# Two-layer hybrid trunk: one weight split behind each combination, u's product ahead of the fourth sum, down units behind side pairs

## The chip, the cores and the metric

The kernel runs on one core of a Trainium2 chip. The metric is the device time of one execution in microseconds. Three runs of the kernel before took 917.51, 919.23 and 922.27 us; the median is 919.23. The engines that matter here are PE (matrix multiply), ACT and DVE (elementwise work), and SP, which only issues DMA transfers. Each works through its own list of instructions in the order that was fixed when the program was built, and waits at the head of the list until what that instruction needs is there.

## The reference

```python
for l in range(DEPTH):                                   # DEPTH = 2
    f = _swiglu(_rmsnorm(h, ff1_norm_pre[l]), ff1_w_gate[l], ff1_w_up[l], ff1_w_down[l])
    h = h + 0.5 * _rmsnorm(f, ff1_norm_post[l])
    m = _hybrid_mixer(_rmsnorm(h, mix_norm_pre[l]), w_in[l], ...)   # SSD scan, pooling, block attention
    h = h + _rmsnorm(m, mix_norm_post[l])
    f = _swiglu(_rmsnorm(h, ff2_norm_pre[l]), ff2_w_gate[l], ff2_w_up[l], ff2_w_down[l])
    h = h + 0.5 * _rmsnorm(f, ff2_norm_post[l])

def _swiglu(h, wg, wu, wd):
    return (jax.nn.silu(h @ wg) * (h @ wu)) @ wd
```

There are 256 tokens of width 1024, and the hidden width of an FFN is 2816. Everything is FP32. The change lies in the four FFNs alone: FFN 1 and FFN 2 of each layer, called 01, 02, 11 and 12 below (layer, FFN).

## The kernel before

**Weights.** All weights come in units of 1 MB (a tile of 128 x 2048). SP loads a unit into one of four raw buffers (L85). To keep FP32 results, a unit is split into an upper part in the short matmul format, copied by ACT (L112, `hi`), and the remainder, subtracted by DVE (L113, `lo`). Each split goes in two pieces of 128 x 1024. The activations are split in the same way, and PE multiplies upper by upper, lower by upper and upper by lower. There are five pairs of split buffers. A fixed list of jobs says in which order units are split. `W.pump()` starts loads and splits as long as buffers are free in the program's bookkeeping, and `pump_behind(m)` does the same with the issue held behind instruction m. A scheduler then places what the program text lets it place on each engine's list, so the lists differ from the order of the text.

**FFN.** The hidden width is cut into 11 blocks of 256 columns. Blocks 0 and 1 are computed together and directly. Blocks 4, 7 and 10 are "side pairs" (`ffn_pair`): gate unit g and up unit u, each in two halves of 128 columns (`mm_side`). The blocks 2+3, 5+6 and 8+9 are computed two at a time as a "block of seven" (`ffn_quad`): instead of eight products it forms seven, from sums of weight units and sums of activations. For the block that starts at i, the splits are g1, T1, T2, T3, g2, T4 and u2. T1, T2 and T4 are sums that DVE forms in place from two raw units (L111). Between T1 and the later products, POOL issues a load that adds a further unit into a raw buffer (L117). The products (L554) are combined by DVE in four steps, "combinations" (L581, L582, L591, L592), and from there come the two hidden tiles h1 (L611) and h0 (L618). One hidden tile per block is turned on PE (`turn_tile`, L528). The other is cast by ACT (L505, `send`), transposed by a DMA that SP issues (L509), and taken in by ACT (L517).

Down units d0 to d10 (`mm_rows`, L409) multiply the turned hidden tiles and accumulate in PSUM. They are interleaved: the down units of the preceding blocks are multiplied between the products of the next one, or behind the next side pair.

**PSUM and the side pairs.** Four banks of PSUM serve the products and the pairs. In pairs 4 and 7 the order of use is g first half, g second half, the turned tile, u first half, u second half. So u's second half takes the bank of g's first half and can start only when DVE has added that half up (L362, after ACT's copy of the other part of the bank, L361). Pair 10 turns no tile on PE, and its four halves have four banks.

**The order that the change touches.** In the middle block (i = 5) the jobs run g1, T1, T2, one down unit, T3, g2, T4, u2, and the T4 product is text ahead of u2's. In the last block (i = 8) u2 comes before T4. Behind each combination `W.pump()` may start any number of splits. Behind h1 and h0 too. In the side pairs nothing holds a down unit behind the pair's u, so that the scheduler may put matmuls of a down unit between the two halves of u.

## Time and profile before

| What | Value |
|---|---|
| Runs | 917.51, 919.23, 922.27 us |
| Profiled execution | 919.46 us, span 917.8 us, mean granted clock 0.998 |
| PE busy | 906.6 us (99% of the span), 4600 matmuls |
| DVE busy | 802.0 us (87%) |
| ACT busy | 643.1 us (70%) |
| DMA | 195.74 MB, 213 GB/s on the mean |
| Chain that ended last | PE 88%, DVE 5%, DMA 3% |

Times within the span count from its start. In a row of the timeline stand the start, the time from the first start to the last end of the group, the engine, the line, the operation, the tiles written and read, the number of instructions, and in brackets the idle time before and what ended it. Neighbouring instructions overlap a little in the records: six lower-part subtractions that follow one another take 6.90 us together and 1.22 us each, so one is due every (6.90 - 1.22) / 5 = 1.136 us. FFN 01 lies at about 10 to 190 us of the span, 02 at 275 to 463, 11 at 460 to 640, 12 at 730 to 915.

### The profile page before, as it was taken

How to read it: one execution, taken by the hardware profiler on the slowest of the kernel's cores; microseconds unless marked ns; L12 is line 12 of the kernel's file. 1: busy time of each engine (PE TensorE's matmuls, PEld its weight loads, DVE VectorE, ACT ScalarE, POOL GpSimd, SP SyncE). 2: the span in 40 equal slices, each digit the busy share in tenths (PEclk: the TensorE clock that was granted, in tenths of full speed). 3: DMA queues.
4: the chain of work that ended last, by engine and by line, in shares of the span. 5: the costliest groups of instructions: out<-in, count | busy, mean ns of one | idle time of the engine just before them, and what ended most of it. 6: DMA issues, size and time to landing. Idle time of an engine off the chain costs nothing.

```text
span 917.8 us, 12327 instructions
## 1 busy us (share of the span) xinstructions
PE 906.6 (99%) x4600; PEld 764.7 (83%) x4600; DVE 802.0 (87%) x1068; ACT 643.1 (70%) x1019; POOL 29.9 (3%) x49
## 2 busy tenths in 40 slices
PE   8999999999999999999999999999999999999997
PEld 5788888889988888888888888888998888888885
DVE  6999889689868999899699989897989699989982
ACT  7767667778738776667765866777795566867681
POOL 0000000000001000000000000000000110000000
PEclk9999999999999999999999999999999999999999
DMA  8567977865534477768655958594824145959651
GB/s 352 164 249 223 365 191 273 256 228 186 183 111 168 120 287 200 275 177 320 207 194 145 343 167 288 155 338 186 297 104 165 65 172 167 348 144 299 198 176 46
DMA packets 49263, 195.74 MB, mean 213 GB/s; under 512 B 24242, under 2 KB 24754, under 8 KB 27188
## 3 DMA queue, kind: packets, MB, share of 16 engines
q1 hardware_dynamic: 47332, 182.24, 56.2%
q0 software_dynamic: 1728, 12.58, 7.5%
q8 instruction: 36, 0.59, 0.3%
q14 instruction: 23, 0.19, 0.1%
q10 hardware_dynamic: 144, 0.13, 0.0%
HBM read 188.65 MB, written 1.05 MB: 207 GB/s over the span
## 4 chain that ended last, share of the span: by engine, by line
PE 88%; DVE 5%; DMA 3%; issue 2%; ACT 1%; POOLq 0%; SPq 0%; POOL 0%; DVEq 0%; ACTq 0%
PE acc L409 27%; PE wk L554 22%; PE wk L387 13%; PE wk L356 9%; PE wk L347 6%; PE wk L358 4%; DVE lo L113 3%; PE wk L374 1%; PE wk L298 1%; DMA raw<-in_ff_q 1%; DMA raw<-in_ff_f 1%; DMA t<-t 1%; PE wk L1047 1%; DMA raw<-in_ff_d 1%; DVE raw L111 1%
## 5 line engine op out<-in xcount | busy, mean ns | idle before, releaser
L112 ACT ACTIVATE hi<-raw 128x1024 fp32r<-128x1024 f32 (+2 forms) x452 | 399.8, 937 | 128.0 <-DMA raw<-in_ff_d 41.8
L113 DVE TENSOR_TENSOR lo<-raw,hi 128x1024 fp32r<-128x1024 f32 (+2 forms) x452 | 464.2, 1077 | 20.0 <-ACT hi L112 19.3
L409 PE MATMUL acc<-hi,t 128*128 128x512 f32 x832 | 216.5, 392 | 1.0 <-ACT hi L112 0.6
L409 PEld LDWEIGHTS acc<-hi,t 128*128 128x128 f32 x832 | 154.1, 188 | 34.4 <-ACT t L247 1.8
L409 PE MATMUL acc<-lo,t 128*128 128x512 f32 x416 | 114.3, 390 | 0.0
L554 PE MATMUL wk<-hi,n 128*128 128x512 f32 x384 | 100.7, 390 | 0.0
L387 PE MATMUL wk<-hi,xT 128*128 128x512 f32 x384 | 98.8, 393 | 0.8 <-ACT hi L112 0.8
L356 PE MATMUL wk<-xT,hi 128*128 128x512 f32 x384 | 97.0, 393 | 0.0
L409 PEld LDWEIGHTS acc<-lo,t 128*128 128x128 f32 x416 | 77.6, 188 | 16.2 <-DVE lo L113 0.2
L111 DVE TENSOR_TENSOR raw<-raw,raw 128x1024 f32<-128x1024 f32 x64 | 76.4, 1217 | 11.0 <-DMA raw<-in_ff_q 11.0
L387 PEld LDWEIGHTS wk<-hi,xT 128*128 128x128 f32 x384 | 71.0, 188 | 16.8 <-ACT hi L112 2.3
L554 PEld LDWEIGHTS wk<-hi,n 128*128 128x128 f32 x384 | 71.8, 188 | 14.8
L356 PEld LDWEIGHTS wk<-xT,hi 128*128 128x128 f32 x384 | 70.0, 188 | 13.3
L554 PE MATMUL wk<-hi,xT 128*128 128x512 f32 x288 | 77.2, 389 | 0.0
L554 PEld LDWEIGHTS wk<-hi,xT 128*128 128x128 f32 x288 | 54.0, 188 | 11.4 <-DVE t L592 0.2
L358 PEld LDWEIGHTS wk<-xT,lo 128*128 128x128 f32 x384 | 52.3, 190 | 3.8
L358 PE MATMUL wk<-xT,lo 128*128 128x256 f32 x384 | 53.5, 282 | 0.0
L554 PE MATMUL wk<-lo,n 128*128 128x512 f32 x192 | 51.6, 390 | 0.5 <-DVE lo L113 0.5
L387 PE MATMUL wk<-lo,xT 128*128 128x512 f32 x192 | 51.5, 390 | 0.0
L554 PEld LDWEIGHTS wk<-lo,n 128*128 128x128 f32 x192 | 36.0, 188 | 8.4 <-DVE lo L113 0.9
L347 PE MATMUL wk<-xT,hi 128*128 128x256 f32 x320 | 42.5, 283 | 0.0
L387 PEld LDWEIGHTS wk<-lo,xT 128*128 128x128 f32 x192 | 36.0, 188 | 7.6
(185 smaller groups left out, 912.2 us busy)
## 6 DMA issues: line engine op xcount, KB each, us to landing
raw<-in_ff_q SPq DMA_DIRECT2D x48, 1024.0 KB, 6.4
raw<-in_ff_d SPq DMA_DIRECT2D x44, 1024.0 KB, 5.4
raw<-in_ff_f SPq DMA_DIRECT2D x16, 1024.0 KB, 6.4
raw<-in_ff_q POOLq DMA_DIRECT2D x12, 1024.0 KB, 8.0
raw<-in_ff_g SPq DMA_DIRECT2D x12, 1024.0 KB, 4.8
raw<-in_ff_u SPq DMA_DIRECT2D x12, 1024.0 KB, 5.0
raw<-in_w_in SPq DMA_DIRECT2D x10, 1024.0 KB, 6.0
raw<-in_w_kvz SPq DMA_DIRECT2D x8, 1024.0 KB, 6.4
```

Source lines behind the costliest of these rows:

```text
L111: nc.vector.tensor_tensor(raw[:, s], self.raw[x][:, s], self.raw[y][:, s], op=op)
L112: self.act = nc.scalar.activation(hi[:, s], raw[:, s], AF.Copy)
L113: nc.vector.tensor_tensor(lo[:, s], raw[:, s], hi[:, s].bitcast(F32), op=ALU.subtract)
L298: pre_turn.last = nc.tensor.transpose(ps[:, k * P : (k + 1) * P], xn[i][:, k * P : (k + 1) * P], ident)
L347: nc.tensor.matmul(ps, w[:, k, s], y[:, k, :], start=i == 0 and k == 0, stop=i == 2 and k == KD - 1)
L356: nc.tensor.matmul(ps, hi[:, k, s], both[:, :, k, :], start=k == 0, stop=k == KD - 1)
L358: nc.tensor.matmul(ps[:, S:], lo[:, k, s], xT[0][:, k, :], start=False, stop=k == KD - 1, skip_group_check=True)
L374: nc.tensor.matmul(ps, x[:, k, s], w[:, k, :], start=i == 0 and k == 0, stop=i == 2 and k == KD - 1)
L387: m = nc.tensor.matmul(ps, y[:, k, :], w[:, k, :], start=h == 0 and n == 0, stop=h == 1 and n == len(parts) - 1)
L409: m = nc.tensor.matmul(acc[b], x[:, j, s], w[:, j, b * 512 : (b + 1) * 512], start=first and j == 0 and i == 0, stop=last and j == 1 and i ...
L554: nc.tensor.matmul(ps, x[:, k, :], w[:, k, :], start=first and n == 0, stop=n == len(parts) - 1, skip_group_check=not first)
L1047: scan.last = nc.tensor.matmul(ps[:, s], decay[t, hd // 4][:, n * P : (n + 1) * P], xdt[t][:, s], start=True, stop=True)
```

## The change

The program text changes in five places.

1. In the middle block u2's job stands ahead of T4's, and u2's product ahead of T4's, as it was in the last block already.
2. In the middle block each pump behind a combination, behind the silu of g2 and behind h0 starts one split at most, and its issue is held behind that combination. In the last block the pump behind g2's silu is cut to four held buffers, with one split, and the one behind h0 to three held buffers. In the first block (i = 2) the pump behind h0 is held behind h0.
3. In the middle and the last block the pump behind h1 is held behind the cast that sends h1 (L505 before, L510 in the changed kernel).
4. In the first block (i = 2) the sum T2 is formed whole (L133) before its splits.
5. In the side pairs all matmuls of the down units are held behind the last matmul of u.

The matmuls are the same 4600 in both kernels, and so are the splits, the sums and the loads. What differs is their order. Line numbers rise by 2 to 12 in the changed kernel: the splits are L114 and L115, the pairs' matmuls L359 and L361, their copy and addition L364 and L365, the down units L412, the products L559, the combinations L586 to L599, silu of g2 L608, silu for h1 L619, h1 L620, h0 L630.

```diff
     def split_next(self, only=None):
+        if i in self.whole:
+            self.sum_next()
...
-    def pump(self, most=SPLIT_BUFS):
+    def pump(self, most=SPLIT_BUFS, splits=10**6):
         while True:
             if self.loaded < len(self.units) and self.live < RAW_BUFS and self.allowed > 0:
                 self.load()
-            elif self.split < len(self.jobs) and self.held < most and self.ready():
+            elif self.split < len(self.jobs) and self.held < most and splits and self.ready():
                 self.split_next()
+                splits -= 1
...
-                late = i == QUADS[-1]
+                if i == QUADS[0]:
+                    W.whole.add(p["T2", i])
+                late, swap = i == QUADS[-1], i != QUADS[0]
...
-                if late:
+                if swap:
                     p["u2", i] = W.job(u2, free=(u2,))
                 p["T4", i] = W.job(g1, (g1, ALU.add, g2), free=(g1, g2))
...
         m = nc.vector.tensor_tensor(pc, pc, w2, op=ALU.subtract)
         if late:
             pump_behind(m, SPLIT_BUFS - 1)
+        elif swap:
+            pump_behind(m, SPLIT_BUFS, 1)
         else:
             W.pump()
...
         m = nc.vector.tensor_tensor(h1, h1, pd, op=ALU.subtract)
         if late:
             pump_behind(m)
+        elif swap:
+            pump_behind(m, SPLIT_BUFS, 1)
         else:
             W.pump()
...
-        W.pump()
+        W.pump(SPLIT_BUFS - late, 1 if swap else 10**6)
...
             hf[1] = send(h1) if by_dma else h1
-            W.pump()
-
-        if not late:
+            if swap:
+                pump_behind(send.last)
+            else:
+                W.pump()
+
+        if not swap:
             second()
         product(pc, left["S4"], p["u2", i], False)
-        nc.vector.tensor_tensor(h0, pc, h0, op=ALU.mult)
+        m = nc.vector.tensor_tensor(h0, pc, h0, op=ALU.mult)
         hf[0] = send(h0) if late and by_dma else h0
-        W.pump()
+        if not late:
+            pump_behind(m, SPLIT_BUFS, 1 if swap else 10**6)
+        else:
+            W.pump(SPLIT_BUFS - 2)
+        if swap:
+            second()
         if late:
-            second()
             downs[0]()
...
-        def both(i):
-            down(i, 0)
+        def both(i, behind=None):
+            down(i, 0, behind)
...
             if i in PAIRS:
                 hT[i] = ffn_pair(i, p, turn, take, by_dma)
+                u = mm_side.end.ins
                 for b in before:
-                    both(b)
+                    both(b, u)
```

Three places show how the lists change. All are of FFN 12.

DVE, from the end of the middle block to side pair 7, before. lo_7692 is the down unit d5, lo_7718 is d6, lo_7739 is g1 of block 8; t_7579 is h1, t_7689 is h0; the two L362 rows add up the two halves of g of pair 7.

```order
766 L592 TENSOR_TENSOR t_7579<-t_7579,wk_7654 128x512
767 L113 TENSOR_TENSOR lo_7670<-raw_7595,hi_7669 128x1024
768 L113 TENSOR_TENSOR lo_7692<-raw_7597,hi_7691 128x1024 x2
769 L113 TENSOR_TENSOR lo_7718<-raw_7620,hi_7717 128x1024
770 L611 TENSOR_TENSOR t_7579<-t_7579,t_7564 128x512
771 L113 TENSOR_TENSOR lo_7718<-raw_7620,hi_7717 128x1024
772 L618 TENSOR_TENSOR t_7689<-wk_7566,t_7689 128x512
773 L113 TENSOR_TENSOR lo_7739<-raw_7652,hi_7738 128x1024 x2
774 L362 TENSOR_TENSOR t_7744<-wk_7745,t_7744 128x256
775 L362 TENSOR_TENSOR t_7744<-wk_7764,t_7744 128x256
```

The same stretch of DVE's list with the change; lo_7711 is d6.

```order
758 L599 TENSOR_TENSOR t_7579<-t_7579,wk_7654 128x512
759 L115 TENSOR_TENSOR lo_7670<-raw_7593,hi_7669 128x1024 x2
760 L115 TENSOR_TENSOR lo_7692<-raw_7618,hi_7691 128x1024 x2
761 L630 TENSOR_TENSOR t_7689<-wk_7566,t_7689 128x512
762 L115 TENSOR_TENSOR lo_7711<-raw_7620,hi_7710 128x1024 x2
763 L620 TENSOR_TENSOR t_7579<-t_7579,t_7564 128x512
764 L115 TENSOR_TENSOR lo_7739<-raw_7652,hi_7738 128x1024 x2
765 L365 TENSOR_TENSOR t_7744<-wk_7745,t_7744 128x256
766 L365 TENSOR_TENSOR t_7744<-wk_7764,t_7744 128x256
```

h1 has moved from the middle of d6's split to behind it. The whole of pair 7's u (lo_7670) now stands behind the last combination; before, its first piece stood ahead of it.

ACT at the same place, before and with the change. L505 and L510 are the cast that sends h1; hi_7738 is the upper part of g1 of block 8.

```order
676 L112 ACTIVATE hi_7717<-raw_7620 128x1024 x2
677 L610 ACTIVATE t_7564<-wk_7654 128x512
678 L112 ACTIVATE hi_7738<-raw_7652 128x1024
679 L505 ACTIVATE t_7711<-t_7579 128x1024
680 L112 ACTIVATE hi_7738<-raw_7652 128x1024
681 L361 ACTIVATE t_7744<-wk_7745 128x256
```

```order
677 L114 ACTIVATE hi_7710<-raw_7620 128x1024 x2
678 L619 ACTIVATE t_7564<-wk_7654 128x512
679 L510 ACTIVATE t_7730<-t_7579 128x1024
680 L114 ACTIVATE hi_7738<-raw_7652 128x1024 x2
681 L364 ACTIVATE t_7744<-wk_7745 128x256
```

Both pieces of g1's upper part now stand behind the cast, and the cast needs h1.

PE in side pair 4, before and with the change. hi_7286 and lo_7287 are u of pair 4, hi_7318 is the down unit d2; wk_7446 is the bank of u's second half.

```order
1660 L528 MATMUL wk_7411<-ident,t_7284 128x128 x4
1661 L356 MATMUL wk_7421<-xT,hi_7286 128x512 x8
1662 L358 MATMUL wk_7421<-xT,lo_7287 128x256 x8
1663 L409 MATMUL acc_7213<-hi_7318,t_7416 128x512
1664 L409 MATMUL acc_7214<-hi_7318,t_7416 128x512
1665 L409 MATMUL acc_7213<-hi_7318,t_7416 128x512
1666 L409 MATMUL acc_7214<-hi_7318,t_7416 128x512
1667 L356 MATMUL wk_7446<-xT,hi_7286 128x512 x8
1668 L358 MATMUL wk_7446<-xT,lo_7287 128x256 x8
```

```order
1656 L533 MATMUL wk_7411<-ident,t_7284 128x128 x4
1657 L359 MATMUL wk_7421<-xT,hi_7286 128x512 x8
1658 L361 MATMUL wk_7421<-xT,lo_7287 128x256 x8
1659 L359 MATMUL wk_7446<-xT,hi_7286 128x512 x8
1660 L361 MATMUL wk_7446<-xT,lo_7287 128x256 x8
1661 L412 MATMUL acc_7213<-hi_7318,t_7416 128x512
1662 L412 MATMUL acc_7214<-hi_7318,t_7416 128x512
```

Four matmuls of d2 have moved from between the halves of u to behind them.

More of the change, by code (lines that the diff above doesn't have):

```diff
@@ L58, in __init__ @@
         self.allowed, self.behind = 10**6, None
-        self.summed = -1
+        self.summed, self.whole = -1, set()
     def unit(self, src, cols=UNIT):
@@ L261, in norm_factor, with pump_behind @@
         return r
-    def pump_behind(ins, most=SPLIT_BUFS):
+    def pump_behind(ins, most=SPLIT_BUFS, splits=10**6):
         with tc.issue_after(ins.ins):
-            W.pump(most)
+            W.pump(most, splits)
     def post(t, f, gain, store=None, end=False):
@@ L357, in mm_side @@
             for k in range(KD):
-                nc.tensor.matmul(ps[:, S:], lo[:, k, s], xT[0][:, k, :], start=False, stop=k == KD - 1,
-                                 skip_group_check=True)
+                mm_side.end = nc.tensor.matmul(ps[:, S:], lo[:, k, s], xT[0][:, k, :], start=False, stop=k == KD - 1,
+                                               skip_group_check=True)
             o = out[:, j * S : (j + 1) * S]
@@ L459, in plan_ffn @@
                     down(before[0])
-                else:
+                if not swap:
                     p["u2", i] = W.job(u2, free=(u2,))
@@ L504, in send @@
         halves = buf(U16, 1024)
-        part = nc.scalar.activation(halves.rearrange("p (a n) -> p a n", a=2),
+        part = send.last = nc.scalar.activation(halves.rearrange("p (a n) -> p a n", a=2),
                                     x[:, :].bitcast(U16).rearrange("p (n a) -> p a n", a=2), AF.Copy)
@@ L558, in ffn_quad @@
     def ffn_quad(i, p, left, turn, downs, by_dma):
-        late = i == QUADS[-1]
+        late, swap = i == QUADS[-1], i != QUADS[0]
         pa = bank()
@@ L612, in second @@
             hf[1] = send(h1) if by_dma else h1
-            W.pump()
-        if not late:
+            if swap:
+                pump_behind(send.last)
+            else:
+                W.pump()
+        if not swap:
             second()
         product(pc, left["S4"], p["u2", i], False)
-        nc.vector.tensor_tensor(h0, pc, h0, op=ALU.mult)
+        m = nc.vector.tensor_tensor(h0, pc, h0, op=ALU.mult)
         hf[0] = send(h0) if late and by_dma else h0
-        W.pump()
+        if not late:
[4 more added lines that the diff above has]
+            second()
         if late:
-            second()
             downs[0]()
@@ L635, in ffn, with down @@
         hf.append(ffn_first(1, p, between=middle if later else None))
-        def down(i, t):
+        def down(i, t, behind=None):
             if acc[t] is None:
                 acc[t] = banks2()
-            mm_rows(acc[t], p["d", i], t, hT[i], i == 0, i == NU - 1)
-        def both(i):
-            down(i, 0)
+            with ExitStack() as order:
+                if behind is not None:
+                    order.enter_context(tc.issue_after(behind))
+                mm_rows(acc[t], p["d", i], t, hT[i], i == 0, i == NU - 1)
+        def both(i, behind=None):
+            down(i, 0, behind)
             if i < NU - TAIL:
-                down(i, 1)
+                down(i, 1, behind)
                 W.done(p["d", i])
```

## The prediction

> **What bounds the kernel now.** I read the busy table and the slices first, then the waits of PE, then the timeline at the places that the change touches.
>
> ```profile
> PE 906.6 (99%) x4600; PEld 764.7 (83%) x4600; DVE 802.0 (87%) x1068; ACT 643.1 (70%) x1019; POOL 29.9 (3%) x49
> PEclk9999999999999999999999999999999999999999
> PE acc L222 <- DVE zeros L211: 2.3, 1, 2.3
> PE wk L387 <- ACT hi L112: 0.8, 1, 0.8
> PE acc L409 <- ACT hi L112: 0.6, 1, 0.6
> PE wk L554 <- DVE lo L113: 0.5, 1, 0.5
> PE acc L409 <- ACT t L247: 0.3, 1, 0.3
> ```
>
> The matrix engine is the bound, at full clock. Without the 2.3 us at the very start it waits 2.2 us in all. The view names waits of a third of a microsecond and more; smaller ones show as starts that come late (d2 at 75.08 below is one), by my estimate 0.7 us more over the four FFNs. So no order of splits can win more than about 3 us (0.3%), since the matmuls stay the same 4600. What the change can lose has no such cap. The question is therefore which matmul will wait that doesn't wait now.
>
> **Part 5, down units behind side pairs: pair 4.** Here are PE and DVE of FFN 12, then the same place in 01, 02 and 11.
>
> ```profile
> 797.49 1.11 PE L358 MATMUL wk<-xT,lo 128*128 128x256 f32 x8
> 798.43 1.16 PE L409 MATMUL acc<-hi,t 128*128 128x512 f32 x4
> 799.43 2.00 PE L356 MATMUL wk<-xT,hi 128*128 128x512 f32 x8
> 796.40 2.36 DVE L113 TENSOR_TENSOR lo<-raw,hi 128x1024 fp32r<-128x1024 f32 x2 [0.52 <-ACT hi L112]
> 798.67 0.75 DVE L362 TENSOR_TENSOR t<-wk,t 128x256 f32<-128x256 f32 x2
> 73.94 1.11 PE L358 MATMUL wk<-xT,lo 128*128 128x256 f32 x8
> 75.08 1.19 PE L409 MATMUL acc<-hi,t 128*128 128x512 f32 x4
> 75.36 0.75 DVE L362 TENSOR_TENSOR t<-wk,t 128x256 f32<-128x256 f32 x2
> 347.93 1.11 PE L358 MATMUL wk<-xT,lo 128*128 128x256 f32 x8
> 349.13 0.75 DVE L362 TENSOR_TENSOR t<-wk,t 128x256 f32<-128x256 f32 x2
> 524.65 1.11 PE L358 MATMUL wk<-xT,lo 128*128 128x256 f32 x8
> 525.01 0.74 DVE L362 TENSOR_TENSOR t<-wk,t 128x256 f32<-128x256 f32 x2
> ```
>
> u's second half needs the bank that the first L362 addition frees. In 12 the first half of u is out at 798.43 (0.94 us after 797.49). The addition starts at 798.67, behind two lower parts of g1 of block 5, takes 0.41 us and frees the bank at 799.08. Before, four matmuls of d2 lay in between, from 798.43 to 799.43, and hid this. With the change nothing covers it. The order on DVE and ACT up to there is the old one, so u's second half waits from 798.43 to about 799.13, and I add 0.1 us for the slow start after a wait (the four of d2 took 1.00 us to the next row; four in stride take 0.91). That is 0.8 less the 0.1 that d2's late start cost: +0.7. In 02 it is 349.54 against 348.88, again +0.7. In 01 it is 75.77 against 74.88, so 1.05, less the 0.3 that d2 paid by coming at 75.08: +0.75. In 11 the bank is free at 525.42, u's half ends at 525.59: 0. Sum **+2.2**. Bounds: 0, if g1's lower parts came 0.9 us earlier, and 3 if they came 0.2 us later everywhere.
>
> **Parts 1 to 3, the middle block: pair 7.** Behind the middle block the same bank decides again, and no down unit lay between the halves of u before. Here are ACT, DVE and PE of FFN 12, then ACT and PE of 01, 02 and 11.
>
> ```profile
> 817.86 0.60 ACT L570 ACTIVATE t<-wk 128x512 f32<-128x512 f32 x1 [2.12 <-PE wk L554]
> 818.85 4.86 ACT L112 ACTIVATE hi<-raw 128x1024 fp32r<-128x1024 f32 x5 [0.39 <-DMA raw<-in_ff_q]
> 840.22 1.04 ACT L505 ACTIVATE t<-t 128x1024 uint16<-128x1024 uint16 x1
> 841.17 1.05 ACT L112 ACTIVATE hi<-raw 128x1024 fp32r<-128x1024 f32 x1
> 809.44 6.90 DVE L113 TENSOR_TENSOR lo<-raw,hi 128x1024 fp32r<-128x1024 f32 x6
> 824.60 0.69 DVE L581 TENSOR_TENSOR t<-wk,t 128x512 f32<-128x512 f32 x1
> 825.20 2.35 DVE L113 TENSOR_TENSOR lo<-raw,hi 128x1024 fp32r<-128x1024 f32 x2
> 843.72 0.74 DVE L362 TENSOR_TENSOR t<-wk,t 128x256 f32<-128x256 f32 x2
> 845.49 2.00 PE L356 MATMUL wk<-xT,hi 128*128 128x512 f32 x8
> 95.62 4.86 ACT L112 ACTIVATE hi<-raw 128x1024 fp32r<-128x1024 f32 x5 [0.49 <-DMA raw<-in_ff_q]
> 122.17 2.00 PE L356 MATMUL wk<-xT,hi 128*128 128x512 f32 x8
> 369.96 4.86 ACT L112 ACTIVATE hi<-raw 128x1024 fp32r<-128x1024 f32 x5 [1.07 <-DMA raw<-in_ff_q]
> 396.10 2.00 PE L356 MATMUL wk<-xT,hi 128*128 128x512 f32 x8
> 545.42 4.86 ACT L112 ACTIVATE hi<-raw 128x1024 fp32r<-128x1024 f32 x5
> 572.57 2.00 PE L356 MATMUL wk<-xT,hi 128*128 128x512 f32 x8
> ```
>
> Before, the first L362 ends at 844.13, 1.36 us ahead of u's second half at 845.49. With the change I walk along DVE from H, the start of g2's upper part (818.85), with 1.14 us for a piece of 1024 and 0.60 for one of 512 (825.20 - 824.60). First lower piece of g2: H + 1.1, when its upper piece is out. Then four pieces of g2 and u2 (4.5), two combinations (1.2), T4's sum (2.3), four pieces of T4 and g7 (4.5), two combinations (1.2), four pieces of u7 and d5 (4.5), h0 (0.6), d6 (2.3), h1 (0.7). That is 22.9. Now DVE has to wait: g1 of block 8 gets its upper part only behind the cast of h1, 0.95 us (841.17 - 840.22), and then one ACT piece of 1.05, both with their releases of 0.05. Its two lower pieces follow (2.3) and the addition (0.4). The bank is free at H + 27.8, where before it was free at H + 25.3. Two microseconds of these 2.5 are the wait for ACT.
>
> The wait at pair 4 moves PE, and so the wanted time. It moves H only where L570, which waits for PE, comes to press on g2's upper part: in 12 ACT idled 0.39 us there, so 0.7 later PE means H 0.2 later; 0.15 in 01 (0.49 idle), 0 in 02 (1.07 idle) and in 11 (PE not late). Bank against wanted time, with 0.05 release and 0.1 slow start:
>
> - 12: 846.9 against 846.2 (845.49 + 0.7): +0.8.
> - 01: 123.6 against 122.9: +0.8.
> - 02: 397.8 against 396.8: +1.1.
> - 11: 573.2 against 572.6: +0.8.
>
> Sum **+3.5**. Bounds: 0, if the walk is 0.9 us too long per FFN; 6, if it is 0.6 too short. The T4 product itself, which the last combination has to precede, is due in 12 ahead of T4's own 12 matmuls (2.7), g7 (5.6), the turned tile (0.3) and u7's first half (2.9), so 11.5 before 846.2, at 834.7; the walk has the last combination done at H + 14.9 = 834.0: no wait.
>
> **Last block and pair 10.** The lateness is carried on: T1's sum in block 8 comes some 2 us later, hence POOL's load behind it, hence T3. The tightest is FFN 11:
>
> ```profile
> 601.12 6.90 DVE L113 TENSOR_TENSOR lo<-raw,hi 128x1024 fp32r<-128x1024 f32 x6
> 619.17 1.09 PE L409 MATMUL acc<-hi,t 128*128 128x512 f32 x4
> 174.90 0.73 PE L409 MATMUL acc<-hi,t 128*128 128x512 f32 x2 [0.34 <-ACT t L247]
> ```
>
> g10's second lower piece ended at 605.75 (the fourth of the six) and will at 607.9. Then h0 (0.6), its cast (0.95), silu for h1 (0.55), h1 (0.7), its cast (0.95), and only then on ACT six upper pieces of u10, d8 and d9 (5.7), two copies of the pair, 0.64, the receipt of the sent tile (1.25), one piece of d10 (0.95) and the split of that tile (0.6): 620.9. d8 wants it at 619.17 + 0.8: +1.0 in 11. The same sum leaves 0.1 in 12 and 0.6 to spare or more in 01 and 02. Against it, both tiles are sent and transposed ahead of the next stage's weights, which takes away in 01 the wait of d10 in the last row, 0.34 with its slow start of 0.1: -0.5. Sum +0.5; bounds -0.5 and +3.
>
> **Part 4, T2's sum whole, and the waits that exist.** In 01 T2 waits 0.5 us for a lower part. If the new order brings that sooner, the d1 unit behind it is no sooner, since its upper part waited for its transfer, and PE stood at it till 55.05:
>
> ```profile
> 42.62 0.73 PE L554 MATMUL wk<-lo,n 128*128 128x512 f32 x2 [0.51 <-DVE lo L113]
> 43.19 1.09 PE L554 MATMUL wk<-hi,n 128*128 128x512 f32 x4
> 53.94 6.75 ACT L112 ACTIVATE hi<-raw 128x1024 fp32r<-128x1024 f32 x7 [5.73 <-DMA raw<-in_ff_d]
> ```
>
> The first of these pieces is out at 55.0, at the same time as before. So 0, bounds -0.7 and +0.4. The wait for ACT's upper part in 11 (0.8) hangs on a load as well and isn't touched.
>
> The sum: 2.2 + 3.5 + 0.5 = +6.2 us on the profiled execution of 919.46 (span 917.8 and 1.7 around it, which stays). That execution lies 0.23 over the median of the runs, so against the median of 919.23 the changed kernel comes to 925.4 (+0.67%).
>
> **The rivals.** About 0.5% (4.6 us) is what a measurement of this kernel tells from no change.
>
> *Pair 7 holds, pair 4 pays.* If the cast's wait is shorter than I walk it, because h1 comes earlier on DVE, the 1.36 us that 12 has to spare now and the 0.7 by which PE is late swallow the rest. Needed: 0.9 us off the 27.8. For it: the walk has some thirty steps. Against it: four FFNs with different loads give the same answer. Then +2.2 + 0.5: 921.9.
>
> *Not slower at all.* The bank of g's first half comes in time at both pairs. The place is DVE's queue ahead of the addition; the point from which it decides is 0.7 us at pair 4 and 0.9 at pair 7. Then only the gains stay, 0.5 in pair 10 and up to 0.7 at T2: 918.0 to 918.7. Against it: the pair 4 part needs no walk, only the old rows with the cover taken away.
>
> *The delay feeds on itself.* Each FFN's block 8 starts over 2 us late, and DVE (87% busy) has little idle time to catch up; if the 1.0 of FFN 11 appears in all four, +3 more, and with the pair 7 bound +2.5 more: 930.9.
>
> *The clock falls.* A wait for a bank could cost more than itself if PE came back slower. In the rows above two matmuls after a 0.51 us wait take 0.57 us to the next row, only 0.1 more than two in stride (0.45). Were the second half of u (2.8 us) to run at half speed after each of the seven new waits, that would be +20: 945. [...] This trace speaks against it for waits of this size, with full clock in every slice.
>
> **How the numbers follow.** Forecast with its neighbourhood 0.5, pair 7 holding 0.23, not slower 0.13, feeding on itself 0.13, the clock 0.01. Slower by over 0.5% means above 923.8: most of the forecast (0.45 of 0.5), the last two, and a little of the second: 0.61. Faster by over 0.5% would need more than the 3 us that there are: 0.02. The rest, 0.37, is no change. The forecast alone spans 922.5 to 928; the range that holds 8 in 10 takes in most of the not-slower case and part of the worse one: 918.8 to 929.5.
>
> **What would show it.** In the waits of PE there should be a new entry, L359 waiting for DVE at L365, some seven times, 0.6 to 1 us each, in pairs 4 and 7. DVE should idle about 2 us for ACT ahead of g1 of block 8, right after h1. The wait for L247's successor L250 should shrink at FFN 01's d10. If L359 has no wait of that kind, the prediction is wrong at its first step; if only pair 4 has it, at the walk.

## The result, and the profile after

The changed kernel takes 927.82 us (median of 6 runs, 925.91 to 929.20) against 919.64 (6 runs, 917.32 to 922.27): the ratio is 1.0086, with a 95% interval of 1.0071 to 1.0102, or 8.2 us more. The forecast was 925.4 with a range of 918.8 to 929.5. The profiled execution has a span of 926.2 us, where before it was 917.8.

Here are the busy times, the granted clock, PE's waits (engine, line, what it waited for, total, number, longest) and the group of DVE's lower parts, of the changed kernel.

```profile
PE 909.8 (98%) x4600; PEld 764.5 (83%) x4600; DVE 803.2 (87%) x1068; ACT 640.1 (69%) x1019; POOL 29.9 (3%) x49
PEclk9999999999999999999999999999999999999999
PE wk L359 <- DVE t L365: 4.9, 6, 1.1
PE acc L225 <- DVE zeros L214: 2.3, 1, 2.3
PE wk L559 <- DVE t L599: 0.8, 1, 0.8
PE acc L412 <- ACT hi L114: 0.7, 2, 0.5
PE acc L412 <- ACT t L250: 0.5, 1, 0.5
PE wk L390 <- ACT hi L114: 0.2, 1, 0.2
...
L115 DVE TENSOR_TENSOR lo<-raw,hi 128x1024 fp32r<-128x1024 f32 (+2 forms) x452 | 463.7, 1078 | 51.2 <-ACT hi L114 46.0
```

The first wait in the list is new and is the one that the prediction named: u's second half waits for the addition of g's first half, at L365. Below the start-up wait, a product of T4 waits for its combination, which the prediction had excluded. DVE's idle time ahead of lower parts, 20.0 us before, is 51.2 us, nearly all of it a wait for ACT's upper parts. The row of the kernel before:

```profile
L113 DVE TENSOR_TENSOR lo<-raw,hi 128x1024 fp32r<-128x1024 f32 (+2 forms) x452 | 464.2, 1077 | 20.0 <-ACT hi L112 19.3
```

DVE has no more work than before (803.2 us against 802.0). Its idle time as a whole grows far less than this one row, from 115.8 us (917.8 - 802.0) to 123.0 (926.2 - 803.2): much of the wait for upper parts stands in the place of other waits. What counts is where it stands.

The place of the first wait, pair 7 of FFN 12, from the timelines of ACT, DVE and PE:

```profile
825.62 3.89 ACT L114 ACTIVATE hi<-raw 128x1024 fp32r<-128x1024 f32 x4
848.30 0.69 DVE L620 TENSOR_TENSOR t<-t,t 128x512 f32<-128x512 f32 x1
849.02 1.06 ACT L510 ACTIVATE t<-t 128x1024 uint16<-128x1024 uint16 x1 [2.74 <-DVE t L620]
849.98 1.99 ACT L114 ACTIVATE hi<-raw 128x1024 fp32r<-128x1024 f32 x2
851.88 0.64 ACT L364 ACTIVATE t<-wk 128x256 f32<-128x256 f32 x2
851.05 2.36 DVE L115 TENSOR_TENSOR lo<-raw,hi 128x1024 fp32r<-128x1024 f32 x2 [2.07 <-ACT hi L114]
853.33 0.75 DVE L365 TENSOR_TENSOR t<-wk,t 128x256 f32<-128x256 f32 x2
851.84 1.11 PE L361 MATMUL wk<-xT,lo 128*128 128x256 f32 x8
853.81 2.11 PE L359 MATMUL wk<-xT,hi 128*128 128x512 f32 x8 [0.86 <-DVE t L365]
```

h1 (L620) ends, DVE idles 2.07 us until ACT has cast h1 and made the first piece of g1's upper part, then come g1's lower pieces and the addition. The addition also needs ACT's copy of the bank (L364), which stands on ACT behind the same cast and both upper pieces. The bank is free at 853.74 (853.33 + 0.41), 28.1 us after the start of g2's upper part at 825.62. PE comes 1.03 us late: eight steps of L361 take 0.94, so it wanted to start at 852.78. With the slow start behind it (the eight matmuls of L359 take 2.11 us, and those of L356 took 2.00 here before) this is 1.1 us. The other three FFNs lose 1.1 to 1.2 us here in the same way.

Pair 4 of FFN 12, DVE and PE, and the T4 product of the middle block of FFN 02, ACT, DVE and PE:

```profile
802.93 2.36 DVE L115 TENSOR_TENSOR lo<-raw,hi 128x1024 fp32r<-128x1024 f32 x2 [0.16 <-ACT hi L114]
805.21 0.75 DVE L365 TENSOR_TENSOR t<-wk,t 128x256 f32<-128x256 f32 x2
805.68 2.11 PE L359 MATMUL wk<-xT,hi 128*128 128x512 f32 x8 [1.11 <-DVE t L365]
...
371.54 3.90 ACT L114 ACTIVATE hi<-raw 128x1024 fp32r<-128x1024 f32 x4 [1.02 <-DMA raw<-in_ff_q]
386.21 0.69 DVE L599 TENSOR_TENSOR t<-t,wk 128x512 f32<-128x512 f32 x1
387.05 1.16 PE L559 MATMUL wk<-hi,xT 128*128 128x512 f32 x4 [0.84 <-DVE t L599]
```

Taken from the starts of the rows, with the slow starts and less what the same place lost before, PE loses:

| Place | 01 | 02 | 11 | 12 | Sum | Predicted |
|---|---|---|---|---|---|---|
| u's second half, pair 4 | 0.1 | 0.3 | 0.5 | 1.3 | 2.2 | 2.2 |
| T4's product, middle block | 0 | 1.1 | 0 | 0 | 1.1 | 0 |
| u's second half, pair 7 | 1.2 | 1.2 | 1.1 | 1.1 | 4.6 | 3.5 |
| d8 to d10, pair 10 | 0.2 | 0 | 0.7 | 0 | 0.9 | 0.5 |
| T2 and d1, first block | -0.1 | 0 | -0.4 | 0 | -0.5 | 0 |

That is 8.3 of the 8.4 us between the two spans. The rest is small: 0.2 won at the start, 0.1 lost in block 8 of 01 and 0.3 in and around the mixers, which fits within the rounding. In pair 10 d8 waits 0.6 us in 01 and 0.4 in 11, several late starts of d10 add 0.2 and 0.3, and d10's old wait in 01 is gone, which wins 0.6.

### The profile page after: what moved, and what is told of

It is laid out like the page before. It is cut to its first block, busy times and chain, and to the rows that moved or that the text cites. A ratio compares the mean times of both kernels' runs of the same rounds, so it can differ in the third digit from the quotient of the medians.

```text
span 926.2 us, 12319 instructions
## 1 busy us (share of the span) xinstructions
PE 909.8 (98%) x4600; PEld 764.5 (83%) x4600; DVE 803.2 (87%) x1068; ACT 640.1 (69%) x1019; POOL 29.9 (3%) x49
## 4 chain that ended last, share of the span: by engine, by line
PE 63%; DVE 17%; DMA 8%; ACT 7%; issue 5%; DVEq 0%; POOLq 0%; SPq 0%; POOL 0%; ACTq 0%
PE acc L412 21%; PE wk L390 13%; DVE lo L115 12%; PE wk L559 11%; PE wk L350 6%; ACT hi L114 5%; DMA raw<-in_ff_q 4%; PE wk L359 3%; DMA raw<-in_ff_d 2%; PE wk L361 2%; PE wk L377 1%; PE wk L301 1%; DMA raw<-in_ff_f 1%; PE wk L1067 1%; DVE raw L113 1%
## 5 line engine op out<-in xcount | busy, mean ns | idle before, releaser
L115 DVE TENSOR_TENSOR lo<-raw,hi 128x1024 fp32r<-128x1024 f32 (+2 forms) x452 | 463.7, 1078 | 51.2 <-ACT hi L114 46.0
L114 ACT ACTIVATE hi<-raw 128x1024 fp32r<-128x1024 f32 (+2 forms) x452 | 397.6, 936 | 124.8 <-DVE raw L113 39.4
L412 PE MATMUL acc<-hi,t 128*128 128x512 f32 x832 | 216.8, 392 | 1.3 <-ACT hi L114 0.7
L412 PEld LDWEIGHTS acc<-hi,t 128*128 128x128 f32 x832 | 153.9, 188 | 35.3 <-ACT t L250 2.4
L412 PE MATMUL acc<-lo,t 128*128 128x512 f32 x416 | 114.2, 390 | 0.0
L359 PE MATMUL wk<-xT,hi 128*128 128x512 f32 x384 | 97.5, 396 | 5.1 <-DVE t L365 4.9
L559 PE MATMUL wk<-hi,n 128*128 128x512 f32 x384 | 100.5, 390 | 0.0
L412 PEld LDWEIGHTS acc<-lo,t 128*128 128x128 f32 x416 | 77.9, 188 | 16.5 <-DVE lo L115 0.2
L359 PEld LDWEIGHTS wk<-xT,hi 128*128 128x128 f32 x384 | 69.6, 188 | 19.9 <-DVE t L365 6.7
L559 PEld LDWEIGHTS wk<-hi,n 128*128 128x128 f32 x384 | 71.8, 188 | 14.8
L559 PE MATMUL wk<-hi,xT 128*128 128x512 f32 x288 | 77.2, 390 | 0.8 <-DVE t L599 0.8
L113 DVE TENSOR_TENSOR raw<-raw,raw 128x1024 f32<-128x1024 f32 x56 | 66.1, 1218 | 0.0
L559 PEld LDWEIGHTS wk<-hi,xT 128*128 128x128 f32 x288 | 53.8, 188 | 12.7 <-ACT t L608 1.2
L361 PEld LDWEIGHTS wk<-xT,lo 128*128 128x128 f32 x384 | 52.3, 190 | 3.9
L361 PE MATMUL wk<-xT,lo 128*128 128x256 f32 x384 | 53.4, 282 | 0.0
L559 PE MATMUL wk<-lo,n 128*128 128x512 f32 x192 | 51.4, 389 | 0.0
L559 PEld LDWEIGHTS wk<-lo,n 128*128 128x128 f32 x192 | 36.0, 188 | 7.6
```

Of the source, the lines that this page charges most:

```text
L113: nc.vector.tensor_tensor(raw[:, s], self.raw[x][:, s], self.raw[y][:, s], op=op)
L114: self.act = nc.scalar.activation(hi[:, s], raw[:, s], AF.Copy)
L115: nc.vector.tensor_tensor(lo[:, s], raw[:, s], hi[:, s].bitcast(F32), op=ALU.subtract)
L359: nc.tensor.matmul(ps, hi[:, k, s], both[:, :, k, :], start=k == 0, stop=k == KD - 1)
L361: mm_side.end = nc.tensor.matmul(ps[:, S:], lo[:, k, s], xT[0][:, k, :], start=False, stop=k == KD - 1, skip_group_check=True)
L412: m = nc.tensor.matmul(acc[b], x[:, j, s], w[:, j, b * 512 : (b + 1) * 512], start=first and j == 0 and i == 0, stop=last and j == 1 and i ...
```

## The experiments

Times are against runs of the kernel before on the same chip; microseconds stand for ratio times 919.6. "A row of the kernel" is one of its profiled execution.

**Down units free again (part 5 undone).**

```diff
-                    both(b, u)
+                    both(b)
```

> The change without its part 5: down units are again free to stand between the halves of u. PE has four matmuls of d2 between the halves of u in pair 4 again, in all four FFNs; everything else is as in the change. Theory (each wait of PE is paid for itself): the waits of u's second half in pair 4, 2.7 us in the changed kernel's trace (0.4, 0.3, 0.55 and 1.4 with the slow starts), go down to some 0.3 in all, pair 7 keeps its 1.1 us per FFN, and the time is about 2.3 us below the change: 925.5. Rival (PE only waits for a late chain of DVE, and a wait saved early is paid later): pair 7 or the T4 product of the middle block waits longer by what pair 4 waits less, and the time stays at 927.8.

Measured: ratio 1.0039 (1.0021 to 1.0057), +3.6 us; 924.58 us. The change lost 8; this one gives 4 of it back, more than the 2.3 of the theory and the opposite of the rival. A trace of the same kernel was taken with a further run:

> The kernel of the run with down units free, once more, for a trace at full clock. The time of that kernel came out 3.2 us below the change by the medians, more than the 2.3 expected. Theory: pair 4 has no wait and pair 7 has 1.1 us in each FFN, as in the change. Rival, to explain the surplus: pair 7's waits are shorter as well (0.5 or less in one FFN or more), because d2's split buffers come free 0.9 us earlier and with them d4's split and g2's load.

That execution took 924.49 us. ACT and PE of its FFN 12 at pair 7:

```profile
847.32 1.99 ACT L114 ACTIVATE hi<-raw 128x1024 fp32r<-128x1024 f32 x2
849.74 0.60 ACT L250 ACTIVATE t<-wk 128x512 fp32r<-128x512 f32 x1
850.39 1.19 PE L412 MATMUL acc<-hi,t 128*128 128x512 f32 x4 [0.81 <-ACT t L250]
851.42 1.99 PE L359 MATMUL wk<-xT,hi 128*128 128x512 f32 x8
```

Pair 4 has no wait over 0.2 us. In pair 7 the scheduler has put four matmuls of d5 between the halves of u, and now they wait, for the turned tile's split (L250), which stands on ACT behind g1's upper part. The place and the cause are the same and the wait has another name. It is 0.97 us here, 0.92, 1.04 and 0.40 in 01, 02 and 11. So the rival of the second run is half right: shorter in one FFN. The rest of the surplus is d8, which doesn't wait in this trace, and T4's product in 02, which doesn't either: the scheduler has put three matmuls of pair 7 ahead of it, as in the kernel before.

**Splits behind h1 not held behind the cast (part 3 undone in the middle block).**

```diff
-            if swap:
+            if late:
                 pump_behind(send.last)
```

> The change with the splits behind h1 in the middle block no longer held behind the cast that sends h1 (the last block keeps its hold). On ACT both upper pieces of g1 of block 8 then stand ahead of the cast. Theory: DVE's 2 us of idle time ahead of g1's lower pieces goes, the bank of g's first half in pair 7 is free about 2 us earlier, so the wait of u's second half there (1.02 to 1.07 us and 0.11 of slow start in each FFN, 4.6 in all) goes to zero, and block 8 starts earlier, which takes away d8's waits too (1.1 us in 01 and 11): about 922.5, between 922 and 923.5. Rival (DVE's queue is late in any case, by the order that puts u2 and T4's sum ahead): the wait for ACT only shrinks, pair 7 still waits 0.5 us or more, 925.5 or above.

Measured: 1.0043 (1.0023 to 1.0064), +4.0; 924.42 us. DVE and PE of FFN 02:

```profile
393.32 0.69 DVE L620 TENSOR_TENSOR t<-t,t 128x512 f32<-128x512 f32 x1
393.92 2.35 DVE L115 TENSOR_TENSOR lo<-raw,hi 128x1024 fp32r<-128x1024 f32 x2
396.19 0.75 DVE L365 TENSOR_TENSOR t<-wk,t 128x256 f32<-128x256 f32 x2
386.14 1.17 PE L559 MATMUL wk<-hi,xT 128*128 128x512 f32 x4 [0.99 <-DVE t L599]
397.76 2.00 PE L359 MATMUL wk<-xT,hi 128*128 128x512 f32 x8
```

g1's lower pieces follow h1 at once, the bank is free at 396.60, 1.2 us ahead of u's second half, and pair 7 has no wait in any FFN. That part of the theory holds to the letter. The time fell by 3.9, not by 5.3: T4's product in 02 still waits 1 us, and d8 and d10 of 02 and 12 start late in this trace, by 1.2 and 0.8 us against the kernel before (0.6 us of it by name, at d8).

**Both undone.**

```diff
-            if swap:
+            if late:
                 pump_behind(send.last)
...
-                    both(b, u)
+                    both(b)
```

> Both of these edits: down units free, and the splits behind h1 of the middle block not held behind the cast. Theory of separate waits: the gains add up, 2.3 and 5.3: about 920.2, within 0.3% of the kernel before. Rival of one late chain: less than the sum, 922 or more.

Measured: 1.0036 (1.0018 to 1.0054), +3.3; 923.73 us. The two gains of 4.3 and 3.9 do not add up; together they give 4.6. The trace has no wait at L365 or at a T4 product of the middle block, and PE's waits beyond start-up are

```profile
PE acc L412 <- ACT t L250: 1.0, 2, 0.5
PE acc L412 <- ACT hi L114: 0.7, 1, 0.7
```

the received tiles of pair 10 and d1. That execution took 921.38 us, 2.35 below the median of its kernel, so it shows less than the kernel loses as a rule. The rival of one late chain is right on the sum: the two holds seem to take from the same spare time.

**Part 5 alone on the kernel before.**

```diff
+                u = mm_side.end.ins
                 for b in before:
-                    both(b)
+                    both(b, u)
```

> The kernel before with part 5 alone: the down units of a side pair are held behind u. Theory: pair 4 pays what the old rows say, 0.7 to 0.8 us in 01, 02 and 12 and nothing in 11, pair 7 has 1.4 us to spare and pays nothing: +2.2 against the kernel before, about 921.9. Rival: the scheduler or the shifted down units make up for it, and the time is that of the kernel before (919.6) within 0.5 us; or pair 7 loses its spare time as well, and it is +4 or more.

Measured: 1.0011 (0.9992 to 1.0031), +1.0 (-0.7 to +2.9); 921.44 us. DVE and PE of pair 4, FFN 12:

```profile
797.67 0.75 DVE L362 TENSOR_TENSOR t<-wk,t 128x256 f32<-128x256 f32 x2
798.15 2.11 PE L356 MATMUL wk<-xT,hi 128*128 128x512 f32 x8 [0.36 <-DVE t L362]
```

The wait is where it was expected, 0.53 us and 0.1 of slow start here, 0.43 and 0.1 in 01, and under 0.2 in 02 and 11. It is about half of the size, in an execution of 919.22 us, 2.2 below the median of its kernel. The interval holds both the 2.2 and nothing, so only the place is shown, not the size.

**The last block's edits alone.**

```diff
-        W.pump()
+        W.pump(SPLIT_BUFS - late, 1 if late else 10**6)
...
-            W.pump()
+            if late:
+                pump_behind(send.last)
+            else:
+                W.pump()
...
         hf[0] = send(h0) if late and by_dma else h0
-        W.pump()
+        W.pump(SPLIT_BUFS - 2 * late)
```

> The kernel before with the change's edits of the last block alone (the pump limits behind g2's silu and behind h0, and the splits behind h1 held behind its cast). Theory: by the walk of the prediction the list on ACT takes 13.0 us from g10's second lower piece to the split of the received tile, which is in time for d8 where block 8 isn't late (0.4 to 1.3 us to spare in the four FFNs), and d10's wait in 01 goes: 0.5 to 0.7 us faster than the kernel before, 919.1. Rival: these edits hold what is left over when the middle block's hold and part 5 are undone (923.7 against 919.7), since d8 and d10 wait there: +2 to +4.

Measured: 0.9994 (0.9983 to 1.0006); 919.27 us. Neither a gain nor a loss that can be told, as the theory had it; the rival is out.

**The middle block's new order alone.** The kernel before with parts 1 and 2 of the middle block, no hold behind the cast and none of down units, last block and first block as before.

```diff
-                if late:
+                if swap:
                     p["u2", i] = W.job(u2, free=(u2,))
...
-            W.pump()
+        elif swap:
+            pump_behind(m, SPLIT_BUFS, 1)
```

> The kernel before with the middle block's new order alone: u2's job and product ahead of T4's, one split behind each combination, no hold behind the cast, no hold of down units, the last block and T2's sum as before. Theory: pair 7 is in time without the hold (the bank is free 26.1 us after g2's upper part starts, not 28.1), but T4's product, which now follows u2's at once, comes before its combination: the last combination ends 15.4 us after g2's upper part starts, PE wants it 16.1 us after the copy of T3's neighbour starts, and the two stand 0.5 to 1.7 us apart: waits of 0.35 in 12, 0.5 in 01, 1.05 in 02, none in 11: +1.9, about 921.6. Rival: the new order by itself costs nothing or wins, 919.7 or below, and the loss is all in the holds and the last block.

Measured: 1.0065 (1.0043 to 1.0086), +6.0; 926.13 us. This is the largest single effect and three times what was expected. First DVE at the middle block of FFN 12 and DVE and PE at its last block, then the same last block in the kernel before:

```profile
829.48 4.63 DVE L115 TENSOR_TENSOR lo<-raw,hi 128x1024 fp32r<-128x1024 f32 x4 [3.70 <-ACT hi L114]
885.24 0.69 DVE L597 TENSOR_TENSOR t<-t,wk 128x512 f32<-128x512 f32 x1
886.08 1.16 PE L557 MATMUL wk<-hi,xT 128*128 128x512 f32 x4 [0.52 <-DVE t L597]
```

```profile
818.92 1.23 DVE L111 TENSOR_TENSOR raw<-raw,raw 128x1024 f32<-128x1024 f32 x1 [2.58 <-DMA raw<-in_ff_q]
872.64 0.69 DVE L592 TENSOR_TENSOR t<-t,wk 128x512 f32<-128x512 f32 x1
875.51 1.07 PE L554 MATMUL wk<-hi,xT 128*128 128x512 f32 x4
```

Before, DVE began T4's sum as soon as g2 had landed, while ACT made the upper parts: 2.58 us idle. Now it waits 3.70 us for g2's upper part and forms T4's sum later, among work that runs without a gap. Before, the last combination of the last block was done at 873.33, 2.2 us ahead of T4's product; now at 885.93, and PE, due at 885.40, waits. The theory had looked for the waits in the middle block itself, where this trace has none; pair 7 has none either. PE loses 2.2, 1.2 and 0.8 us in block 8 of 01, 02 and 12, and nothing in 11, at the products of u2 and T4.

How the order brings this about is not shown. The lateness of DVE is part of it: POOL's load behind T1 is issued up to 1.1 us later against PE's work than before. But in 01, where PE loses most, it is only 0.1 later. What goes with the loss is the time that this load takes to land: 11.6, 10.6, 9.0 and 10.2 us in 01, 02, 11 and 12, against 8.0, 8.0, 9.5 and 8.7 before. It varies without the new order too (10.5 in 11 with the order of the products alone, below). The execution also is the slowest of its kernel, 930.32 us, 4.2 above the median. In its pair 10 of 01 d8 waits 2.96 us for a received tile, and PE is slow for 6 us behind that (last section), 5.1 us in all against the kernel before.

**The hold behind the cast alone.**

```diff
-            W.pump()
+            if i == QUADS[1]:
+                pump_behind(send.last)
+            else:
+                W.pump()
```

> The kernel before with one edit: the splits behind h1 in the middle block are held behind the cast that sends h1. On ACT both the cast and the silu then stand ahead of d6's and g1's upper pieces. Theory: g1's lower pieces, and with them the addition that frees the bank in pair 7, come 1.65 us later than before; the old spare times were 1.36 us in 12, 1.06 in 01, 0.82 in 02 and 2.1 in 11, so waits of 0.45, 0.7, 0.95 and 0 us: +2.1, about 921.8. Rival 1: the hold hurts only together with the new order of the middle block: 919.7. Rival 2: the hold by itself costs what pair 7 pays in the change, +4.6: 924.3.

Measured: 1.0021 (1.0007 to 1.0035), +1.9; 921.27 us. The size is the theory's 2.1; both rivals lie outside the interval. The cause shows in one FFN alone. At pair 7 of 01 PE waits 0.50 us for the turned tile's split, which stands on ACT behind g1's upper part, and 0.17 for the bank. 02 and 12, where the theory had 0.95 and 0.45, don't wait at pair 7; 02 waits 0.5 us in pair 4, ahead of its hold. The longest wait is at d8 in pair 10 of 01:

```profile
173.80 1.66 PE L409 MATMUL acc<-hi,t 128*128 128x512 f32 x4 [2.21 <-ACT t L247]
```

That execution took 926.17, 4.9 us above the kernel's own time, so the row shows more than the hold costs as a rule, and the agreement in size may be luck.

**One cause taken away: g1 split behind the additions.**

```diff
-                pump_behind(send.last)
+                pump_behind(send.last, SPLIT_BUFS - (not late))
             else:
-                W.pump()
+                W.pump(SPLIT_BUFS - 1)
...
-            pump_behind(m, SPLIT_BUFS, 1 if swap else 10**6)
+            pump_behind(m, SPLIT_BUFS - 1, 1 if swap else 10**6)
```

> The change with one cause taken away: in the first and the middle block the pumps behind h1 and h0 may hold four jobs instead of five, so that g1 of the next block of seven is split only behind the additions of pair 4's and pair 7's g. The hold behind the cast, the hold of the down units and the new order all stay. Theory of the bank (u's second half waits because the addition that frees its bank stands on DVE behind g1's lower pieces): both waits of PE at L365, 4.9 us in the changed kernel's list and 7.3 with the unnamed part and slow starts, go to under 0.5, and the time falls by about as much, to 921 or 922. Rival of one late chain: PE waits elsewhere instead, at the T4 products, at d8 or d10, and the time stays above 924.

Measured: 1.0124 (1.0107 to 1.0141), +11.4; 930.78 us. PE's longest waits, one of them on PE's timeline, and POOL's load behind T1's sum in FFN 11; then that load in the changed kernel:

```profile
PE wk L559 <- DVE wk L587: 5.6, 4, 1.5
PE wk L559 <- DVE t L599: 2.7, 4, 0.7
606.75 1.20 PE L559 MATMUL wk<-hi,n 128*128 128x512 f32 x4 [1.41 <-DVE wk L587]
585.88 0.86 POOL L119 DMA_DIRECT2D raw<-in_ff_q  x1 [46.56 <-DVE raw L113]
```

```profile
581.48 0.86 POOL L119 DMA_DIRECT2D raw<-in_ff_q  x1 [46.92 <-ACT hi L114]
```

There is no wait at L365 left, in pair 4 or 7: the bank explains those. But T1's sum is formed in g1's raw buffer and has to follow g1's split, so POOL's load is issued 4.4 us later (4.1 against PE's work, in each of the four FFNs), T3 is late, and u2's and T4's products of block 8 wait for their combinations in all four FFNs. The rival of one late chain is right on the time. The edit takes the wait away and pays more elsewhere, by a delay of its own; what the change would cost with the wait gone and nothing else moved, it doesn't show.

**The old order with all the holds.** The change with parts 1 and 2 undone in the middle block.

```diff
-                if swap:
+                if late:
                     p["u2", i] = W.job(u2, free=(u2,))
...
-        late, swap = i == QUADS[-1], i != QUADS[0]
+        late, swap = i == QUADS[-1], i == QUADS[-1]
...
-            if swap:
+            if i != QUADS[0]:
                 pump_behind(send.last)
```

> The change with its parts 1 and 2 undone in the middle block: u2's job and product behind T4's again, and no limit of one split. The hold behind the cast of h1, the hold of the down units, T2's sum whole and the last block's edits stay. Theory (the holds by themselves cost what they cost alone): 1.0 for the down units, 2.0 for the cast, nothing for the rest, +2.5 to +3 on the kernel before, about 922.3; what is left to 927.8 is then the new order's share, over 5 us. Rival: the holds alone make the loss, since pairs 4 and 7 wait for the same addition in any order: 926 or more.

Measured: 1.0021 (1.0009 to 1.0032), +1.9; 921.75 us. DVE and PE of FFN 12 at pair 7:

```profile
842.80 4.63 DVE L115 TENSOR_TENSOR lo<-raw,hi 128x1024 fp32r<-128x1024 f32 x4 [2.07 <-ACT hi L114]
847.35 0.75 DVE L365 TENSOR_TENSOR t<-wk,t 128x256 f32<-128x256 f32 x2
848.03 2.00 PE L359 MATMUL wk<-xT,hi 128*128 128x512 f32 x8
```

DVE idles the same 2.07 us behind h1, and yet the bank is free at 847.76, 0.27 us before PE wants it. PE waits for this addition in pair 7 of no FFN. So pair 7's wait needs both: the hold without the new order (here) and the new order without the hold (above) leave it at nothing. What this trace loses is in pair 4, 1.7 us against the kernel before, where part 5 acts. The rival is out; the 1.9 lies below the theory's 2.5 to 3, at the edge of the interval. The new order's share of the loss is 8 - 1.9, about 6, what it also costs alone.

**T2's sum whole, alone.**

```diff
+                if i == QUADS[0]:
+                    W.whole.add(p["T2", i])
```

> The kernel before with part 4 alone: T2's sum in the first block formed whole, ahead of its splits. Theory of the prediction: the wait of T2's product in 01 for a lower piece (0.67 us and 0.11) goes, d1 behind it waits as much longer for its transfer, nothing changes: 919.4. Rival: the earlier start is kept: 918.7; or the DVE list is put off by the whole sum: 920.5.

Measured: 0.9997 (0.9985 to 1.0009); 919.87 us. T2's wait is gone, and d1 starts 0.77 us late instead of 0.06. Nothing changes, as predicted; the time alone couldn't tell this from the first rival's 918.7, the trace does. The second rival is out.

**The order of the products alone.**

```diff
-        if not late:
+        if i == QUADS[0]:
             second()
         product(pc, left["S4"], p["u2", i], False)
...
-        if late:
+        if i != QUADS[0]:
             second()
```

> The kernel before with the products of the middle block alone exchanged in the program text: u2's ahead of T4's, while the jobs (the order of splits) and the pumps stay. PE's list stays as it was in FFN 12, where the scheduler had u2 ahead of T4 already; h1 moves behind d6's lower pieces on DVE. The middle block's new order without holds had cost 6 us. Theory: that cost lies in the order of the splits (T4's sum now begins only behind u2's lower pieces and two combinations, where it used to fill DVE's wait for g2's upper part), not in the order of products: within 1 us of the kernel before, 919.6. Rival: the later h1 and its cast make the loss: 923 or more.

Measured: 1.0008 (0.9992 to 1.0023), +0.7; 920.01 us. The scheduler had put u2's product ahead of T4's on PE already (all of it in three FFNs, ten of twelve matmuls in 01). The later h1 is out as the cause. What is left is the order of the splits on ACT and DVE, together with the limit of one split behind each combination; no run takes these two apart.

No version came out faster than the kernel before. The two closest are the last block's edits alone and T2's sum alone, both within 0.15% of it.

## Why the prediction was right, and where it was off

**PE is the bound and there is little to win.** Right. No experiment gained anything that can be told, and what the change lost is waits of PE at full clock. The view of waits names smaller ones than the third of a microsecond that the prediction took for its limit (0.17 in the hold alone); this changes nothing in the sum.

**Part 5, pair 4: +2.2.** The sum in the trace is 2.2, but the FFNs differ (0.1, 0.3, 0.5 and 1.3 against 0.75, 0.7, 0 and 0.7). The step took the landings of loads from one execution and kept them for all. Ahead of g1's upper part ACT waited 1.23, 2.17, 0.44 and 0.89 us for its load before, and 0.97, 1.37 and 1.46 in 01, 02 and 11 with the change; in 12 the down unit ahead of it came late (0.91 us of waiting at 799.31). Whether the change itself moved them was not tried. Part 5 alone measured +1.0, with an interval that reaches from nothing to 2.9. Place and mechanism are shown, the size is not.

**Parts 1 to 3, pair 7: +3.5.** Measured 4.6; mechanism right, and the term mis-sized by 1.1. The walk from g2's upper part to the free bank gave 27.8 us and the trace has 28.1 in all four FFNs; over four FFNs that is about the 1.1. The 2 us of idle time ahead of g1 are 2.07. Most of the missing 0.3 are combinations that read what the one before them wrote: the walk counted 0.60 us for each, and each second one comes after 0.72. T4's sum adds 0.16: its lower parts start 2.43 us after it (832.58 to 835.01) and not 2.27, since ACT's upper part comes between. The walk took ACT's list in its order, and in this trace ACT kept to it: its copy of g's first half (L364), whose bank PE had filled by 846.91, did not pass the cast for which ACT idled 2.74 us until 849.02, and started at 851.88, behind both upper pieces of g1.

**"The T4 product ... no wait".** This step failed. It was worked out for 12 alone. The last combination ends 15.35 us after g2's upper part starts in all four FFNs, and not 14.9, so that 01, 11 and 12 have 0.28 us left and not the 0.7 that the step had. In 02, g2's load lands a microsecond after the copy that the other FFNs wait for (1.02 us idle at 371.54), and the last combination ends at 386.90. T4's product, due at 386.05, starts 1.0 us late, 1.1 with its slow start (1.16 us for its first four matmuls, 1.07 for the four that end ahead of the wait). The row of 02 that the prediction shows had this idle time (1.07) before. The cover is gone as well: before, the scheduler had three matmuls of pair 7 between the products of u2 and T4 in 02, 11 and 12, and with the change T4's follows at once.

**Last block: +0.5.** Measured 0.9. The wait of d8 that was expected in 11 (1.0) is 0.4 there and 0.6 in 01, where the step had seen time to spare; late starts of d10 add 0.5, and d10's old wait in 01 is gone as predicted.

**Part 4: nothing.** Right in 01, by the mechanism given: d1 took over T2's wait. In 11, d1 came 0.8 us late before and 0.4 with the change, which the step had left as it was; why is not shown.

**The sum.** 6.2 were forecast and 8.2 measured; pair 7 and T4 make the difference, 1.1 each, and the 0.4 more in pair 10 and the 0.5 won at d1 and T2 cancel. What the sum hid is that its terms are not separate. Undoing part 5 gave 4.3 us back, undoing the hold 3.9, undoing both 4.6. The reading that fits is that the change spends the spare time of one chain, DVE's and ACT's work from block 5 through pair 10, and PE pays where it runs out first. The rival in which the delay feeds on itself had named the carrying-over, but not its size: block 8 and pair 10 lose 1.0 us in the trace where it had 3.5. The largest spender is the new order in the middle block, +6.0 alone, with waits in block 8 in its trace that no step of the prediction priced; with the last block's edits beside it, T2's sum and the first block's hold behind h0, it is +3.3 (both holds undone). That the whole came out within 2.4 us of the forecast is in part luck: a sum of separate terms was the wrong form for it.

**The clock.** The rival of the falling clock is out for the change: with a dozen waits of 0.2 to 1.1 us the granted clock is 0.999 and every slice shows full clock. The half speed in this rival was the author's assumption; the trace of the kernel before shows full clock in every slice. In two other runs PE was slow behind a longer wait: the granted clock was 0.50 behind 2.96 us and behind 2.21 us (last section).

**What stays open.** Why the last block's edits, worth nothing alone, make the new middle order 2.7 us cheaper was not taken apart, and the intervals (1.7 to 5.0 and 4.0 to 7.9) overlap. Their order on ACT sends both tiles early, and the traces fit that: without these edits d8 in 01 waits 2.96 us (new order alone), 2.21 (hold alone) and 1.80 (T2's sum alone) for a received tile, and not by name in three other traces; with them it waits 0.5 at most, in seven traces. What makes the new order dear, and why the hold costs 1.9 by itself but shows no wait in pair 7 beside the other holds in the old order, is open too. The first block's hold behind h0 was never run alone.

## What to carry to other kernels

Where one engine is full and another feeds it in a fixed order, price a new order along the feeding engine's whole list up to the next place where it has time to spare, and not only at the first wait that it makes. Note which work fills a wait for a transfer: T4's sum had done that, and the order that moved it into a stretch without gaps cost more than both holds, though that the sum's place made the cost is argued and not shown. And a wait that PE shows can be only where the chain comes out; before mending it, ask what stands behind it in the same queue. Terms of one chain need not add up: 4.3 and 3.9 us gave 4.6 here. And look where in the spread of its kernel's runs a traced execution lies, before its longest wait is taken for the cause.

## What the hardware showed that was not expected

DVE rows of the changed kernel, FFN 02, at the first two combinations:

```profile
377.18 0.68 DVE L586 TENSOR_TENSOR t<-wk,t 128x512 f32<-128x512 f32 x1
377.90 0.70 DVE L587 TENSOR_TENSOR wk<-wk,t 128x512 f32<-128x512 f32 x1
378.51 2.35 DVE L113 TENSOR_TENSOR raw<-raw,raw 128x1024 f32<-128x1024 f32 x2
```

The second combination reads what the first wrote and starts 0.72 us after it; the sum behind it reads nothing of it and starts after 0.61. In these rows instructions of 128x512 overlap by some 0.08 us where they are independent and not at all where they are not (0.04 us lie between the end of the first, at 377.86, and the start of the second). Two such pairs stand in the walk to pair 7, and 2 x 0.12 us is most of the 0.3 that it lacked.

PE in pair 10 of FFN 01, in the run of the new order alone: the row of d8, and the stretch from 174 to 180 us with the busy time of each engine, the granted clock (third from the end), the DMA share and GB/s:

```profile
174.33 2.08 PE L412 MATMUL acc<-hi,t 128*128 128x512 f32 x4 [2.96 <-ACT t L250]
174.00:180.00 6.00, 5.67 (x13) 4.46 (x14) 4.96 (x9) 5.41 (x10) 0.00 (x0) 0.50 1.06 389
```

After this wait of 2.96 us the granted clock is 0.50 for six microseconds, and the matmuls come 0.43 us apart and not 0.23, which costs 2.8 us on top of the wait. In the run of the hold alone, the 2.21 us shown above are followed by 0.50 from 174.4 to 177.6, 1.6 us on top. After 1.80 us at the same place, with T2's sum alone, the clock stays at 1.00, as it does behind the 2.3 us at the very start. So the rival of the falling clock had a place here after all, for waits about twice as long as the change makes; each of the three was seen in one execution.
